# The last projections of 512 tokens: three kept weight tiles in two halves, or two passes over all eight tiles

## The chip, the cores and the metric

The kernel runs on one core of a Trainium2 chip. The metric is the device time of one execution in microseconds (us). A core has five engines, each of which works through its own instructions in order: TensorE (PE) for matmuls, VectorE (DVE), ScalarE (ACT), GpSimd (POOL) and SyncE (SP), which here issues nearly all DMAs. Engines wait for each other by semaphores.

## The reference

Two models of two layers each follow each other on 256 context and 256 latent tokens of width 1024, in float32. Cut to what the change touches, a layer is

```python
h = modulate(rms(x), shift, scale)            # context and latents have their own shift, scale, gate
x = x + gate * rms(mixer(h) @ w_out)          # second model: x + gate * (mixer(h) @ w_out)
h = modulate(rms(x), shift2, scale2)
x = x + gate2 * rms(ffn(h) @ w_down)          # second model: x + gate2 * (relu(h @ w1)**2 @ w2)
```

The mixers are gated linear attention with grouped attention, HGRN, latent attention with retention, and S5 (a state-space scan). The layers that still need the context compute w_out and w_down for all 512 tokens; the others for the 256 latents alone.

## The kernel before

Activations lie with the 1024 features on 8 x 128 partitions and the tokens in the free dimension, context in columns 0 to 255 and latents in 256 to 511. A float32 product is made of three matmuls of parts: `mm3` (L207) multiplies, for each block k of 128 input features, hi x xh, hi x xl and lo x xh, where hi is the rounded weight and lo its rest. `load` (L263) brings one weight tile, 128 output features by all of k, 512 KB (448 KB with seven blocks), by a DMA on SP into one of 4 `raw` buffers; `split` (L199) casts it to `hi` on ACT (L203) and subtracts to `lo` on DVE (L204), each with 3 buffers. The result of a tile goes to a bank of PSUM with the tag `pl`, of which there are 3, and `consume` evicts it from there.

`linear_steps` (L221) loops over the weight tiles. With `ends` set and N = 512 it does tiles 0 to 2 in two halves of 256 columns, tiles 3 and 4 at 512 columns, and then takes the last three together: it loads and splits them, does the context half of all three, calls `half()`, and does the latent half of all three. `half()` is where the context goes on while the latents are still being multiplied. Four places set `ends`:

- S1, about 344 to 400 us: `ew_out`, the output of the even mixer. `consume` copies to y (L1789) and adds the squares (`add_squares`: square L77 on ACT, sum by a matmul L85). `half()` is the first step of `halves` (L519): the rstd of the context's rows (cp L102, sums L105, eleven small DVE steps L420 to L428, spread over partitions by L119 on PE), then x += y * vecP * rstd tile by tile (L515 on DVE, L516 on GpSimd or DVE) with the squares of the new x. After the projection the same is done for the latents, and then the normalized X of both (L494 to L500), from which the ffn's matmuls read.
- S2, 790 to 836 us: `f0_d2`, the last of three down blocks of the first ffn, with seven blocks of k. `consume` adds to y (L1735). `half()` and what follows are as in S1.
- S3, 1711 to 1770 us: `bw_out`, the output of the second model's first mixer. `consume` (L1878) is x += gate * psum; x is loaded just before, from `ctx2` (L1872) and from the stored latents (L1873), into the place of tiles that the mixer used. M (L1046 on ACT, L1047 on DVE) is the mixer's output and the projection's input. `half()` is the context's rstd.
- S4, 2100 to 2149.6 us: `p0_d3`, the last of four down blocks of the third ffn. `consume` adds to y (L1735) and to x (L1909); `s5_collect` scales x to u (L1544), writes u of the tile to memory once its latent columns are there (L1547), and after tiles 3 and 7 gathers it back as U in eight DMAs (L1551). `s5_u` scales U (L1560, L1561), and the S5 scan (st, L1637 to L1641) works on what is computed from U.

The order of the instructions on each engine is not that of the code: a list scheduler sets it from priorities and dependences, and each engine then works in that order. Background streams that the loops advance with `tick` (here "w" and "m") have ended before these places' tiles are done.

## Time and profile before

| | us |
|---|---|
| median of three runs (2506.3 to 2512.42) | 2507.03 |
| the profiled execution's own time | 2504.24 |
| its span, first to last instruction | 2502.5 |
| PE busy in it | 2370.1 |
| DVE busy | 1499.1 |
| ACT busy | 967.3 |
| GpSimd busy | 453.7 |

The mean granted clock of TensorE is 0.971 of full speed. Busy times of engines overlap each other. A row of a timeline gives the start, the time, engine, line, operation, what is written and read, and, in brackets, how long the engine was idle before and what ended that; matmuls are pipelined, so their pace is the distance of their starts.

### The profile page before, as it was taken

Reading aid. Unit: us, or ns where it says so; the run is one execution under the profiler, and the core shown is the slowest. Engines: PE = TensorE matmul, PEld = TensorE weight load, DVE = VectorE, ACT = ScalarE, POOL = GpSimd, SP = SyncE. Lnnn points to the kernel's source line nnn. Section 1 sums busy time; section 2 is a strip of 40 time slices with the busy share of each in tenths; the row PEclk is TensorE's granted clock in tenths of the full one; section 3 lists DMA queues with packets and bytes.
Section 4 is the critical chain, followed back from the end, with each engine's and each line's share of the span. In section 5 each row is a group of like instructions: output and inputs, shape, how many; then the busy total and the mean of one; then the engine's idle time right before and its main releaser. Section 6 shows DMA issues by size and latency. Waiting matters only on the chain.

```text
span 2502.5 us, 40056 instructions
## 1 busy us (share of the span) xinstructions
PE 2370.1 (95%) x15813; PEld 1951.2 (78%) x15813; DVE 1499.1 (60%) x2913; ACT 967.3 (39%) x1591; POOL 453.7 (18%) x596
## 2 busy tenths in 40 slices
PE   7999988999999899999999999999999999958999
PEld 5875566888888669987899796557888888628999
DVE  5555446778853646674555633665688734586666
ACT  5523323322223434434444534443423224535543
POOL 3920012556630201101000100110000000360000
PEclk9999998999999899999999999999999999979999
DMA  8336671555552262225755431003365533966554
GB/s 301 114 101 227 228 278 59 162 165 168 158 154 93 80 210 76 72 81 182 264 177 181 160 108 59 9 18 119 118 188 179 165 97 109 221 253 210 168 180 150
DMA packets 162925, 378.05 MB, mean 151 GB/s; under 512 B 24144, under 2 KB 70096, under 8 KB 162608
## 3 DMA queue, kind: packets, MB, share of 16 engines
q1 hardware_dynamic: 159728, 368.27, 46.4%
q0 software_dynamic: 3008, 7.21, 1.0%
q8 instruction: 125, 2.05, 0.3%
q14 instruction: 64, 0.52, 0.1%
HBM read 344.75 MB, written 30.67 MB: 150 GB/s over the span
## 4 chain that ended last, share of the span: by engine, by line
PE 80%; DVE 10%; DMA 4%; ACT 3%; issue 2%; POOL 1%; SPq 0%; DVEq 0%; ACTq 0%; POOLq 0%
PE pl L213 19%; PE pl L214 18%; PE pl L215 18%; PE pm L337 3%; PE pl L993 2%; DVE lo L204 2%; DMA mcol<-ada_t 2%; PE pl L287 1%; PE pl L288 1%; PE pl L285 1%; DVE pm L403 1%; PE pa L669 1%; PE pb L1024 1%; PE pl L1015 1%; PE pa L85 1%
## 5 line engine op out<-in xcount | busy, mean ns | idle before, releaser
L203 ACT CAST hi<-raw 128x1024 fp32r<-128x1024 f32 (+4 forms) x393 | 400.6, 1020 | 841.5 <-PE pl L214 496.7
L204 DVE TENSOR_TENSOR lo<-raw,hi 128x1024 fp32r<-128x1024 f32 (+4 forms) x393 | 489.0, 1246 | 343.8 <-ACT hi L203 341.8
L214 PE MATMUL pl<-X,hi 128*128 128x256 f32 (+1 forms) x2032 | 646.4, 319 | 6.3 <-POOL X L498 5.8
L213 PE MATMUL pl<-X,hi 128*128 128x256 f32 (+1 forms) x2032 | 649.3, 322 | 2.0 <-ACT X L495 1.6
L215 PE MATMUL pl<-X,lo 128*128 128x256 f32 (+1 forms) x2032 | 644.5, 318 | 0.0
L214 PEld LDWEIGHTS pl<-X,hi 128*128 128x128 f32 x2032 | 390.1, 192 | 40.1 <-POOL X L498 8.3
L213 PEld LDWEIGHTS pl<-X,hi 128*128 128x128 f32 x2032 | 389.6, 193 | 40.3 <-issue 9.0
L215 PEld LDWEIGHTS pl<-X,lo 128*128 128x128 f32 x2032 | 389.8, 192 | 31.1 <-issue 4.9
L214 PE MATMUL pl<-hl,hi 128*128 128x256 f32 (+1 forms) x1071 | 327.2, 306 | 6.9 <-DVE hl L1722 6.8
L213 PE MATMUL pl<-hh,hi 128*128 128x256 f32 (+1 forms) x1071 | 327.7, 307 | 3.8 <-ACT hh L1721 3.7
L215 PE MATMUL pl<-hh,lo 128*128 128x256 f32 (+1 forms) x1071 | 325.8, 305 | 0.0
L213 PEld LDWEIGHTS pl<-hh,hi 128*128 128x128 f32 x1071 | 202.4, 189 | 19.8 <-ACT hh L1721 4.8
L214 PEld LDWEIGHTS pl<-hl,hi 128*128 128x128 f32 x1071 | 202.7, 189 | 18.5 <-DVE hl L1722 8.9
L215 PEld LDWEIGHTS pl<-hh,lo 128*128 128x128 f32 x1071 | 203.0, 190 | 10.3 <-issue 0.8
L337 PE MATMUL pm<-mraw,s_cc 128*32 128x512 f32 x576 | 119.2, 622 | 13.4 <-DMA mraw<-ada_w 13.1
L213 PE MATMUL pl<-M,hi 128*128 128x256 f32 (+1 forms) x416 | 122.9, 297 | 6.3 <-ACT hi L203 5.3
L1514 POOL TENSOR_TENSOR Ec<-PGr,bc 128x576 f32<-128x576 f32 x64 | 95.6, 1504 | 169.5 <-DMA bc<-s_w 87.5
L215 PE MATMUL pl<-M,lo 128*128 128x256 f32 (+1 forms) x416 | 122.2, 295 | 1.5 <-DVE lo L204 1.5
L214 PE MATMUL pl<-M,hi 128*128 128x256 f32 (+1 forms) x416 | 122.4, 296 | 0.2 <-DVE M L864 0.2
L498 POOL TENSOR_TENSOR X<-nt,X 128x256 fp32r<-128x256 f32 x48 | 37.9, 789 | 418.4 <-ACT nt L497 418.4
L403 DVE SCALAR_TENSOR_TENSOR pm<-mcol,mrow 128x512 f32<-128x512 f32 x128 | 89.3, 698 | 33.1 <-DMA mcol<-ada_t 22.8
L1735 DVE TENSOR_TENSOR y<-y,pl 128x256 f32<-128x256 f32 (+1 forms) x86 | 45.2, 526 | 102.5 <-PE pl L215 102.1
(513 smaller groups left out, 3629.6 us busy)
## 6 DMA issues: line engine op xcount, KB each, us to landing
mraw<-mod_w SPq DMA_DIRECT2D x96, 512.0 KB, 5.6
raw<-f_u SPq DMA_DIRECT2D x88, 512.0 KB, 4.3
mraw<-ada_w SPq DMA_DIRECT2D x64, 512.0 KB, 6.2
raw<-p_u SPq DMA_DIRECT2D x64, 512.0 KB, 3.7
raw<-p_d SPq DMA_DIRECT2D x64, 512.0 KB, 3.7
raw<-ow_fm SPq DMA_DIRECT2D x32, 512.0 KB, 3.3
mcol<-ada_t SPq DMA_DIRECT2D x64, 256.0 KB, 3.1
raw<-f_d SPq DMA_DIRECT2D x32, 448.0 KB, 3.3
```

The costliest lines, as they stand in the source:

```text
L85: K.nc.tensor.matmul(self.ps[32 * j:32 * j + 32, :N], K.ones[:rows, :32], sq[:rows, :N], start=k < 4, stop=k + 4 >= self.kt, skip_group_ch ...
L203: nc.scalar.copy(hi, raw)
L204: nc.vector.tensor_tensor(lo, raw, f32(hi), ALU.subtract)
L213: mm(out, w[0][:, kw, wsl], xh, start=first and a == 0, stop=False, skip_group_check=True)
L214: mm(out, w[0][:, kw, wsl], xl, start=False, stop=False, skip_group_check=True)
L215: mm(out, w[1][:, kw, wsl], xh, start=False, stop=last and a == nk - 1, skip_group_check=True)
L337: nc.tensor.matmul(ps[32 * j:32 * j + 32, :], s[:, k, :], raw[:, jj * 512:(jj + 1) * 512], start=k == 0, stop=k == KT - 1, skip_group_chec ...
L403: nc.vector.scalar_tensor_tensor(self.psum("pm"), buf[:, n % 2], 1.0, s[:, v], ALU.mult, ALU.mult, accum_out=(dst if h else part)[:, v, j: ...
L498: nc.gpsimd.tensor_tensor(lo[:, k, a:b], t, f32(hi[:, k, a:b]), ALU.subtract)
L993: nc.tensor.matmul(ps[:, :nk], q[:, tt * P:(tt + 1) * P], k[:, :nk], start=True, stop=True)
L1514: nc.gpsimd.tensor_tensor(Ec[i], ff[i], cs[i], ALU.mult)
L1735: nc.vector.tensor_tensor(y[:, c, a0:b0], y[:, c, a0:b0], ps, ALU.add)
```

## The change

With `ends`, the loop now makes two passes over all eight tiles: first the context half of each tile, then `half()`, then the latent half of each. Each pass loads and splits each tile itself and takes a bank for each half. The special case of the last three tiles goes. In `ffn` the flag is set where N is 512 alone, so that the ffns of 256 latents stay as they were.

```diff
--- before.py
+++ after.py
@@ -238,8 +238,18 @@
             self.mm3(ps[:M, :N], w, X, ks[early:], False, True, slice(0, M), slice(xoff, xoff + N))
             consume(first, ps[:M, :N], 0, N)
             yield
-        tail = nt - 3 if N == T and ends else nt
-        for c in range(1 if early else 0, tail):
+        if ends:
+            for a, b in ((0, CTX), (CTX, T)):
+                for c in range(nt):
+                    w, ps = weights(c), self.psum("pl")
+                    self.mm3(ps[:M, a:b], w, X, ks, True, True, slice(0, M), slice(xoff + a, xoff + b))
+                    consume(first + c, ps[:M, a:b], a, b)
+                    self.tick(tick)
+                    yield
+                if a == 0 and half is not None:
+                    half()
+            return
+        for c in range(1 if early else 0, nt):
             w = weights(c)
             ps = self.psum("pl")
             if N == T and c < 3:
@@ -250,15 +260,6 @@
             consume(first + c, ps[:M, :N], 0, N)
             self.tick(tick)
             yield
-        if tail < nt:
-            ws = [weights(c) for c in range(tail, nt)]
-            pss = [self.psum("pl") for _ in ws]
-            for a, b in ((0, CTX), (CTX, T)):
-                for i, (w, ps) in enumerate(zip(ws, pss)):
-                    part(ps, w, a, b)
-                    consume(first + tail + i, ps[:M, a:b], a, b)
-                if a == 0 and half is not None:
-                    half()
 
     def load(self, Wd):
         raw = self.wp.tile(list(Wd.shape), F32, tag="raw", name=self.n("raw"), bufs=4)
@@ -1737,7 +1738,7 @@
                     after(c, a0, b0)
 
             last = b == len(Wd) - 1
-            self.linear_fm(wd, (hi, lo), N, add, tick=ticks[1], ends=last, half=half if last else None)
+            self.linear_fm(wd, (hi, lo), N, add, tick=ticks[1], ends=last and N == T, half=half if last else None)
 
 
 def body(tc, A, out, dbg=None):
```

Instructions as the two kernels issue them: 13814 matmuls become 14000, DVE goes from 2787 to 2834, ACT from 1529 to 1561, SP from 833 to 865, GpSimd stays at 601. The orders of all engines differ inside S1 to S4 alone. Line numbers of the kernel after are one higher from L264 on.

S1 on DVE, from the subtraction of the sixth tile before, and of a tile of the second pass after (`Wt` is a product for the S5 weights, `cp` the start of the context's rstd, `y<-pl` an eviction). Before:

```order
L204 TENSOR_TENSOR lo_3149<-raw_3146,hi_3148 128x1024
L1506 TENSOR_TENSOR Wt_3736<-PGr,bc_3647 128x512
L1789 COPY y_2889<-pl_3074 128x512
L204 TENSOR_TENSOR lo_3155<-raw_3152,hi_3154 128x1024
L1789 COPY y_2889<-pl_3108 128x512
L204 TENSOR_TENSOR lo_3161<-raw_3158,hi_3160 128x1024
L1789 COPY y_2889<-pl_3164 128x256
L1789 COPY y_2889<-pl_3165 128x256
L1789 COPY y_2889<-pl_3166 128x256
L102 COPY cp_3253<-pa_2946 128x256
```

After:

```order
L204 TENSOR_TENSOR lo_3234<-raw_3231,hi_3233 128x1024
L1790 COPY y_2889<-pl_3101 128x256
L204 TENSOR_TENSOR lo_3269<-raw_3266,hi_3268 128x1024
L1507 TENSOR_TENSOR Wt_3758<-PGr,bc_3756 128x512
L1507 TENSOR_TENSOR Wt_3759<-PGr,bc_3756 128x512
L1790 COPY y_2889<-pl_3134 128x256
L1508 TENSOR_TENSOR Wt_3758<-Wt_3758,Wt_3759 128x512
L204 TENSOR_TENSOR lo_3302<-raw_3299,hi_3301 128x1024
L102 COPY cp_3169<-pa_2922 128x256
```

The two products `Wt` and their sum stand between evictions of the context's last tiles, and two subtractions and a sum ahead of `cp`.

S3 on DVE, from the last part of M (`M`) on; `x<-pl` is an eviction that needs x. Before:

```order
L1264 TENSOR_TENSOR rq_13319<-rq_13319,pb_15714 128x512
L1047 TENSOR_TENSOR M_14308<-rq_13319,M_14307 128x512
L204 TENSOR_TENSOR lo_15921<-raw_15918,hi_15920 128x1024
L1878 SCALAR_TENSOR_TENSOR x<-pl_15743,n_7567,x 128x256
L1878 SCALAR_TENSOR_TENSOR x<-pl_15806,n_7567,x 128x256
L204 TENSOR_TENSOR lo_15956<-raw_15953,hi_15955 128x1024
L1878 SCALAR_TENSOR_TENSOR x<-pl_15743,n_7567,x 128x256
L1878 SCALAR_TENSOR_TENSOR x<-pl_15806,n_7567,x 128x256
L1878 SCALAR_TENSOR_TENSOR x<-pl_15865,n_7567,x 128x256 x2
```

After:

```order
L1265 TENSOR_TENSOR rq_13531<-rq_13531,pb_15926 128x512
L1048 TENSOR_TENSOR M_14520<-rq_13531,M_14519 128x512
L204 TENSOR_TENSOR lo_16053<-raw_16050,hi_16052 128x1024
L204 TENSOR_TENSOR lo_16086<-raw_16083,hi_16085 128x1024
L204 TENSOR_TENSOR lo_16124<-raw_16121,hi_16123 128x1024
L1879 SCALAR_TENSOR_TENSOR x<-pl_15955,n_7779,x 128x256
L1879 SCALAR_TENSOR_TENSOR x<-pl_15990,n_7779,x 128x256
L1879 SCALAR_TENSOR_TENSOR x<-pl_16023,n_7779,x 128x256
L1879 SCALAR_TENSOR_TENSOR x<-pl_16056,n_7779,x 128x256
```

Three subtractions stand ahead of the first eviction, and the fourth tile's context half (`pl_16056`) is evicted right behind the first three.

S3 on PE, where the third tile ends and the fourth begins (the first three tiles are `pl_15743`, `pl_15806`, `pl_15865` before and `pl_15955`, `pl_15990`, `pl_16023` after). Before:

```order
L215 MATMUL pl_15865<-M_14307,lo_15862 128x256
L213 MATMUL pl_15865<-M_14307,hi_15861 128x256
L214 MATMUL pl_15865<-M_14308,hi_15861 128x256
L215 MATMUL pl_15865<-M_14307,lo_15862 128x256
L213 MATMUL pl_15924<-M_14307,hi_15920 128x512
L214 MATMUL pl_15924<-M_14308,hi_15920 128x512
```

After:

```order
L215 MATMUL pl_16023<-M_14519,lo_16020 128x256
L213 MATMUL pl_16023<-M_14519,hi_16019 128x256
L214 MATMUL pl_16023<-M_14520,hi_16019 128x256
L215 MATMUL pl_16023<-M_14519,lo_16020 128x256
L213 MATMUL pl_16056<-M_14519,hi_16052 128x256
L214 MATMUL pl_16056<-M_14520,hi_16052 128x256
```

Before, 92 matmuls, both halves of three tiles, stand between the first that needs the last part of M and the fourth tile; after, 20 do. Seven weight loads of this projection stand ahead of the loads of x on SP in both orders.

S4 on SP (`raw<-p_d` is a weight load, `u<-u` a written u, `U<-u` the gather, `wT` weights of S5). Before:

```order
L1547 DMA u<-u_19131 128x512
L265 DMA raw_19454<-p_d 128x1024
L1547 DMA u<-u_19131 128x512
L1619 DMA wT_20005<-tt 128x1024
L1547 DMA u<-u_19131 128x512
L1619 DMA wT_20015<-tt 128x1024
L1915 DMA xd<-x 128x4x256
L1547 DMA u<-u_19131 128x512
L1619 DMA wT_20025<-tt 128x1024
L1551 DMA U<-u 16x32x64 x8
L1547 DMA u<-u_19131 128x512 x4
```

After:

```order
L1548 DMA u<-u_19447 128x512
L266 DMA raw_20052<-p_d 128x1024
L1548 DMA u<-u_19447 128x512
L1620 DMA wT_20430<-tt 128x1024
L1548 DMA u<-u_19447 128x512
L1620 DMA wT_20440<-tt 128x1024
L1916 DMA xd<-x 128x4x256
L1548 DMA u<-u_19447 128x512
L1620 DMA wT_20450<-tt 128x1024
L1548 DMA u<-u_19447 128x512
L1552 DMA U<-u 16x32x64 x8
L1548 DMA u<-u_19447 128x512 x3
```

The fifth tile's u is now written ahead of the gather, and three are left behind it where four were; all weight loads of the second pass but the last stand ahead of the first u.

## Rows read from the trace of the kernel before

**Rows 1.** The page: busy time by engine; the chain's shares by engine.

```profile
PE 2370.1 (95%) x15813; PEld 1951.2 (78%) x15813; DVE 1499.1 (60%) x2913; ACT 967.3 (39%) x1591; POOL 453.7 (18%) x596
...
PE 80%; DVE 10%; DMA 4%; ACT 3%; issue 2%; POOL 1%; SPq 0%; DVEq 0%; ACTq 0%; POOLq 0%
```

**Rows 2.** Timeline of PE at S3: start, us, engine, line, tiles, [idle before].

```profile
1726.93 0.50 PE L213 MATMUL pl<-M,hi 128*128 128x256 f32 x2 [0.65 <-ACT M L1046]
...
1733.04 0.28 PE L214 MATMUL pl<-M,hi 128*128 128x256 f32 x1
...
1733.76 0.28 PE L214 MATMUL pl<-M,hi 128*128 128x256 f32 x1
...
1738.08 0.40 PE L213 MATMUL pl<-M,hi 128*128 128x512 f32 x1
...
1740.14 0.39 PE L213 MATMUL pl<-M,hi 128*128 128x512 f32 x1
```

**Rows 3.** Groups of ACT and DVE instructions by line: busy us, mean ns.

```profile
L203 ACT CAST hi<-raw 128x1024 fp32r<-128x1024 f32 x340 | 356.3, 1049 | 720.7 <-PE pl L214 450.1 <-issue 214.8 <-PE pl L288 25.8
...
L204 DVE TENSOR_TENSOR lo<-raw,hi 128x1024 fp32r<-128x1024 f32 x340 | 433.8, 1277 | 297.4 <-ACT hi L203 295.9
...
L1735 DVE TENSOR_TENSOR y<-y,pl 128x256 f32<-128x256 f32 x52 | 21.9, 421 | 36.7 <-PE pl L215 36.4
```

**Rows 4.** Timelines of DVE and, last, of PE at S1.

```profile
361.21 2.33 DVE L1506 TENSOR_TENSOR Wt<-PGr,bc 128x512 f32<-128x512 f32 x2 [0.18 <-DMA bc<-s_w]
...
365.17 1.20 DVE L1507 TENSOR_TENSOR Wt<-Wt,Wt 128x512 f32<-128x512 f32 x1
...
366.29 2.45 DVE L204 TENSOR_TENSOR lo<-raw,hi 128x1024 fp32r<-128x1024 f32 x1
...
418.34 0.62 PE L213 MATMUL pl<-X,hi 128*128 128x256 f32 x3 [0.51 <-ACT X L495]
```

**Rows 5.** Timelines of DVE, then of PE, behind S2's latent half.

```profile
840.04 0.16 DVE L420 TENSOR_SCALAR ms<-pb 128x2 f32<-128x2 f32 x1 [0.37 <-PE pb L105]
...
841.26 0.16 DVE L423 TENSOR_SCALAR ms<-ms 128x2 int32<-128x2 int32 x1
...
846.35 1.74 PE L85 MATMUL pb<-sq,ones 128*32 128x256 f32 x4 [1.82 <-ACT sq L77]
...
856.01 1.01 PE L213 MATMUL pl<-X,hi 128*128 128x256 f32 x3
```

**Rows 6.** Timelines of DVE and SP (DMA issues, SPq) at S3.

```profile
1726.91 0.69 DVE L1047 TENSOR_TENSOR M<-rq,M 128x512 fp32r<-128x512 f32 x1 [2.06 <-ACT M L1046]
...
1727.99 0.57 SPq L1872 DMA_DIRECT2D x<-ctx  x1
...
1733.75 0.93 DVE L1878 SCALAR_TENSOR_TENSOR x<-pl,n,x 128x256 f32<-128x256 f32 x2 [0.49 <-DMA x<-ctx]
```

**Rows 7.** PE's timeline; then the window: busy by engine, PEclk, DMA share, GB/s.

```profile
344.05 0.58 PE L213 MATMUL pl<-M,hi 128*128 128x256 f32 x1 [5.14 <-ACT hi L203]
...
344.00:350.00 6.00, 5.48 (x25) 5.19 (x26) 3.68 (x3) 2.10 (x2) 0.00 (x0) 0.53 0.79 259
```

**Rows 8.** SP and DVE timelines and one window behind S4's gathers.

```profile
2130.04 5.57 SPq L1551 DMA_DIRECT2D U<-u  x8
...
2140.00:2144.00 4.00, 4.00 (x32) 3.55 (x32) 2.40 (x12) 0.39 (x1) 0.00 (x0) 1.00 1.00 104
...
2149.56 0.42 DVE L1735 TENSOR_TENSOR y<-y,pl 128x256 f32<-128x256 f32 x1 [1.88 <-PE pl L215]
...
2153.78 8.50 SPq L1551 DMA_DIRECT2D U<-u  x8
...
2155.32 0.42 DVE L1560 TENSOR_TENSOR U<-U,pa 128x256 f32<-128x256 f32 x1 [0.18 <-DMA xd<-x]
...
2171.12 0.41 DVE L1560 TENSOR_TENSOR U<-U,pb 128x256 f32<-128x256 f32 x1
...
2173.14 0.50 DVE L1637 TENSOR_TENSOR st<-s5V,s5aa 128x256 f32<-128x256 f32 x1 [1.60 <-ACT s5V L1598]
```

## The prediction

> **What bounds the kernel now.** I read the page first: TensorE (PE) is busy 95% of a 2502.5 us span and 80% of the chain that ended last is PE [rows 1]. So what counts is PE's own instructions and the places where PE waits. The change touches four places, each one projection onto 512 tokens: S1, the output of the even mixer (about 344 to 400 us); S2, the last down block of the first ffn (790 to 836); S3, the output of the second mixer (1711 to 1770); S4, the last down block of the third ffn (2100 to 2149.6). At each I read the PE timeline for waits, then the timelines of the engine that PE waits for, then the order of the instructions before and after. The orders differ inside the four places alone, so I price these four and nothing else.
>
> **Matmuls.** In each place two tiles were done at 512 columns, 24 matmuls for a tile (21 at S2), and are now done in two halves of 256. In [rows 2] the 256-wide ones start 0.12 us apart (1733.04 to 1733.76, six steps) and the 512-wide ones 0.229 (1738.08 to 1740.14, nine steps), so a split costs 2 x 0.12 - 0.229 = 0.011 us. There are 24 x 2 x 3 + 21 x 2 = 186 such splits: 2.1 us, 0.5 in each place, all of it on PE. The Trainium skill (TensorE: Matmul & The Clock Gate, section "Wait — 56ns, not 53.3ns?") puts the spacing at columns over the clock and about 2.5 ns for each matmul; by that the 186 would cost 0.5 us and the sum below would be 1.6 us lower. The rows are of this kernel's own matmuls, and I keep theirs.
>
> **Second loads, casts and subtractions.** Each of the four places loads its eight tiles twice: 32 more loads, 32 casts on ScalarE (ACT, 1.05 us) and 32 subtractions on VectorE (DVE, 1.28 us) [rows 3]. A pass now takes PE 24 x 0.12 = 2.88 us for each tile; DVE needs 1.28 + 0.42 for a subtraction and half an eviction and ACT 1.05 and about as much as that eviction for a square [rows 3]. Both fit, so I price them at nothing by themselves; if the cover goes (a subtraction has taken 2.45 us beside GpSimd work at S1 [rows 4]), DVE's 2.45 + 0.42 just reaches 2.88. What costs is where such an instruction now stands ahead of one that PE waits for.
>
> **S1.** In the new order the weights' product for a later stage (two Wt instructions, 2.33 us; their sum 1.20) stands on DVE ahead of the eviction of the last context tile, and a subtraction ahead of the copy cp that starts the context's rstd chain. Counted from the end of the tile before, DVE has 0.42 + 1.28 + 2.33 = 4.0 us [rows 3, 4] of work against PE's 2.88; PE comes to the sum of squares 8 matmuls (0.96 us) into the latents, and needs an eviction and a square (0.42 each) more: about 1.0 us of waiting. The cp then stands behind 1.20 + 1.28 us while PE has 14 matmuls (1.7 us): 0.9. The rstd steps have another product, an eviction and a subtraction between them, which the 35 matmuls behind them (4.2 us) nearly cover: 0.3. S1: 0.5 + 1.0 + 0.9 + 0.3 = **+2.7** (bounds: 0 if nothing waits and the context's squares, done earlier, give back what the splits cost; +5 if two subtractions take 2.45).
>
> **S2.** One subtraction stood inside the latents' rstd chain: two steps that take 0.16 us start 1.22 us apart, at 840.04 and 841.26 [rows 5]; in the new order the subtraction is done by then, -1.0. On the other hand the sums of squares of the context's x now stand 12 matmuls behind the broadcast of rstd (L119) where they stood 24 behind. The way from L119 over DVE, GpSimd and ACT back to such a sum shows as 1.82 us of idle PE after the pass [rows 5]; twelve matmuls hide 1.4 of it, but DVE has a subtraction in between, so I take it whole, +1.8. S2: 0.5 + 1.8 - 1.0 = **+1.3** (bounds -0.5 and +3).
>
> **S3** is the largest term. The eviction here is x += gate x psum, and x is only loaded here: SP issues the load at 1727.99, behind DVE's M at 1726.91, and DVE has it at 1733.75 [rows 6]. PE gets the last part of M at 1726.93. Before, it then still has both halves of the first three tiles to do, 92 matmuls, and comes to the fourth tile at 1738.08 [rows 2]: the load is hidden. Now only the context half of three tiles stands there; 20 matmuls are left, done by 1726.93 + 20 x 0.12 = 1729.3. The fourth tile needs a bank, the projection has three, and the first comes free when x has landed and 0.48 us later: 1734.3. PE idles 5.0 us. S1 shows what such a hole does next: after 5.14 us of idle PE the granted clock of the next 6 us is 0.53, about the lower of its two levels (1.2 of 2.4 GHz), and 25 matmuls take 5.48 us in place of 3.0 [rows 7]: 2.5 us more. Seven loads of weights stand ahead of x on SP in both orders, so x itself comes no later. S3: 0.5 + 5.0 + 2.5 = **+8.0** (bounds +4.5 without the clock, +9.5).
>
> **S4.** After each latent tile u goes to memory, and after the fourth and the eighth tile a gather of eight DMAs brings U back. Before, all latent halves of the first five tiles come early: the first gather is issued from 2130.04 on, the DMA engines are still full at 2140 to 2144, so it takes some 13.5 us, and it is over when the last tile is evicted at 2149.56 [rows 8]. Now the fourth tile's latent half ends only four tiles (12 us) before the end, its gather is issued some 6.5 us before the end and, at 13.5 us is over about 7 us after it. The first use of U stood 5.8 us after the end (2155.32): +1.5. The last u is written behind that gather in SP's queue and lands about 8 us after the end; the second gather waits for it, was issued at 2153.78 before (4.2 after the end), and is 3.9 us later. Its user ends at 2171.5 and stands on DVE ahead of the scan's first step at 2173.14, which follows it: 1.6 us of slack, so +2.3. I take 2.5 for both together, since they overlap. S4: 0.5 + 0.3 (two more waits at the start) + 2.5 = **+3.3** (bounds +0.8, if the gather is quicker beside fewer loads, and +6, if the loads queued behind it come late for the chain too).
>
> **Sum.** 2.7 + 1.3 + 8.0 + 3.3 = 15.3 us. The profiled execution took 2504.24 us and would take 2519.5; the median of the three runs is 2.8 us above it, so on the median 2507.03 + 15.3 = **2522.3 us**, 0.6% slower.
>
> **Rivals.**
> (a) The two long terms are hidden: x lands before PE runs dry, or the fourth tile's matmuls find a bank, and the gather has slack in the scan. Then S3 is 0.5 and S4 0.8: 2.7 + 1.3 + 0.5 + 0.8 = 5.3, 2512.3 us, no change that can be told (0.3%, 7.5 us, is about what a measurement of this kernel can tell). For it speaks that PE had 11 us of cover before; against, that the order leaves 20 matmuls of it.
> (b) Faster: the latent pass of 23 us, where it was 8.6, hides the context's whole norm chain, so that PE does the context half of the next ffn's first three tiles (72 x 0.12 = 8.6 us) while it now idles after the pass until 418.34 [rows 4] and 856.01 [rows 5], and 3.5 us at S3's end. That is -20.8, with 2.1 + 7.5 + 2.8 still to pay: -8.4, 2498.6 us. It decides if the context's normalized tiles are written before the latents' rstd is asked for. Against it: in the new order these instructions stand on DVE and PE exactly where they stood, behind the latents' own.
> (c) Slower yet: the doubled subtractions meet the residual work on DVE and GpSimd in the latent passes of S1 and S2. If half of the 16 tiles see the 2.45 us, that is 8 x 1.2 = 10 us more: 2532 us. For it speaks [rows 4]; against, that GpSimd works in a few of these tiles only.
>
> **Chances.** Forecast 0.73, (a) 0.14, (b) 0.05, (c) 0.08. Faster by over 0.3%: (b), 0.05. Within 0.3%: (a) and the lowest corner of the forecast, 0.17. Slower: 0.78. The lower bounds of the four places add up to 0 - 0.5 + 4.5 + 0.8 = +4.8, the upper ones to 5 + 3 + 9.5 + 6 = +23.5, 2511.8 to 2530.5; with (a) and half of (c) inside the range is 2511 to 2532, which leaves out (b), the rest of (c) and a little more.
>
> **What would show it.** PE at S3: one idle stretch of about 5 us before the fourth tile, ended by DVE's eviction, and that by the DMA of x, with the clock at half speed behind it; if PE goes on there, S3 falls, and with it the forecast. At S4 the second use of U some 4 us later against the end of the projection, and the scan's first step 2 to 3 us later. At S1 and S2 waits of a microsecond or less at the sums of squares; waits for the subtraction itself tile after tile would be (c). A first ffn matmul that comes 8 us sooner after the pass would be (b).

## The result and the profile after

The changed kernel takes 2526.16 us (median of five runs, 2523.1 to 2531.12) against 2507.6 (2506.3 to 2516.51): a ratio of 1.0075 with a 95% interval of 1.0058 to 1.0093. It is 0.75% slower, 18.8 us (14.5 to 23.3); the forecast was 15.3 us and 2522.3. The same kernel, timed again later, gave 1.0063 [1.0041, 1.0086], 15.8 us.

The page of the changed kernel (its profiled execution took 2531.12 us, span 2529.3), busy time by engine, as the first row of [rows 1]:

```profile
PE 2382.2 (94%) x15999; PEld 1970.2 (78%) x15999; DVE 1542.6 (61%) x2960; ACT 999.3 (40%) x1623; POOL 450.8 (18%) x596
```

PE's busy time grew by 12.1 us and the span by 26.8, so more than half of the loss is PE waiting. DVE has 43.5 us more of work (47 instructions, most of them the second subtractions) and ACT 32.0.

**Where it went.** Two executions of the same code drift against each other, so spans don't tell what a place costs. I took the DVE and ACT instructions that both traces have in the same order, and the median difference of their start times in a stretch just ahead of each place and in one just behind it. What this difference grows by is the cost of the place:

| us | S1 | S2 | S3 | S4 |
|---|---|---|---|---|
| forecast | +2.7 | +1.3 | +8.0 | +3.3 |
| changed kernel | 5.4 | -0.5 | 6.9 | 0.6 |
| changed kernel, second time | 6.8 | -1.1 | 6.5 | 0.6 |

Places that an experiment (below) left as before came out between -1.2 and about +1, so about a microsecond of each number is noise. In stretches where nothing was changed the same difference wandered by several microseconds either way: ahead of S1 it lay between -2.3 and +5.9 in the traces of this study, and +5.5 of the 26.8 us by which this span is longer were there before S1 began.

One stretch of unchanged order does more than wander. Some 60 us behind S2's pass the difference grows by 3.0 us in the first trace of the changed kernel and by 1.9 in the second. PE's rows there, before and in the changed kernel, show a wait for a load of `ada_w`, the weights of the modulation:

```profile
899.64 1.92 PE L337 MATMUL pm<-mraw,s_cc 128*32 128x512 f32 x4 [2.32 <-DMA mraw<-ada_w]
```

```profile
913.97 1.92 PE L338 MATMUL pm<-mraw,s_cc 128*32 128x512 f32 x4 [4.29 <-DMA mraw<-ada_w]
```

The table counts none of this; the experiments show in which kernels it comes.

**S3** is as forecast. PE's timeline, as [rows 2]: start, us, engine, line, tiles, and in brackets the idle time before and what ended it:

```profile
1743.06 0.28 PE L215 MATMUL pl<-M,lo 128*128 128x256 f32 x1
1747.97 0.55 PE L213 MATMUL pl<-M,hi 128*128 128x256 f32 x1 [4.63 <-DVE x L1879]
1748.32 0.41 PE L214 MATMUL pl<-M,hi 128*128 128x256 f32 x1
1748.53 0.41 PE L215 MATMUL pl<-M,lo 128*128 128x256 f32 x1
```

The third tile's context half ends, PE finds no bank, and DVE's eviction frees one 4.63 us later. The eviction itself waits for the load of x, in the timelines of SP and DVE, as [rows 6]:

```profile
1741.43 0.57 SPq L1873 DMA_DIRECT2D x<-ctx  x1
...
1742.91 3.50 DVE L204 TENSOR_TENSOR lo<-raw,hi 128x1024 fp32r<-128x1024 f32 x3 [1.56 <-ACT hi L203]
...
1747.34 1.27 DVE L1879 SCALAR_TENSOR_TENSOR x<-pl,n,x 128x256 f32<-128x256 f32 x3 [0.93 <-DMA x<-ctx]
```

From issue to use it takes 5.91 us, where it was 5.76 [rows 6]: x comes no later, but PE comes earlier. DVE itself stands idle for x in the last 0.93 us only: until 1746.41 it does the three subtractions that the new order puts ahead of the first eviction. In this order an earlier x would have freed the bank at most 0.93 us sooner. And the clock falls behind the hole: the windows give busy us of PE, PEld, DVE, ACT and POOL, the granted clock, the DMA share and GB/s.

```profile
1743.00:1748.00 5.00, 0.37 (x4) 0.20 (x3) 4.07 (x5) 1.86 (x3) 0.00 (x0) 0.74 0.97 319
1748.00:1753.00 5.00, 5.00 (x26) 5.00 (x27) 0.63 (x3) 1.15 (x4) 0.00 (x0) 0.58 1.06 388
1753.00:1758.00 5.00, 5.00 (x46) 4.46 (x45) 3.31 (x4) 2.63 (x4) 0.00 (x0) 1.00 0.71 238
```

After 4.63 us of idle PE the clock of the second window is 0.58, near the lower of the two levels, and 26 matmuls are recorded in five microseconds where 46 follow in the next five.

**S1** cost twice the forecast. PE's waits in its two passes:

```profile
380.52 0.62 PE L85 MATMUL pa<-sq,ones 128*32 128x256 f32 x2 [1.79 <-ACT sq L77]
...
384.07 0.61 PE L105 MATMUL pa<-pack_sb,cp 128*128 128x1 f32 x4 [1.06 <-DVE cp L102]
...
390.79 0.68 PE L119 MATMUL pa<-pack_sb,rs 128*128 128x128 f32 x4 [1.82 <-DVE rs L429]
```

They are the three waits of the forecast, 4.67 us together where 2.2 were expected. The timelines of DVE and GpSimd beside them, as [rows 4], show why:

```profile
376.34 3.35 DVE L1507 TENSOR_TENSOR Wt<-PGr,bc 128x512 f32<-128x512 f32 x2
379.61 0.41 DVE L1790 COPY y<-pl 128x256 f32<-128x256 f32 x1
379.95 1.37 DVE L1508 TENSOR_TENSOR Wt<-Wt,Wt 128x512 f32<-128x512 f32 x1
381.24 2.45 DVE L204 TENSOR_TENSOR lo<-raw,hi 128x1024 fp32r<-128x1024 f32 x1
383.61 0.41 DVE L102 COPY cp<-pa 128x256 f32<-128x256 f32 x1
383.94 1.37 DVE L1507 TENSOR_TENSOR Wt<-PGr,bc 128x512 f32<-128x512 f32 x1
...
385.63 1.00 DVE L424 TENSOR_SCALAR ms<-ms 128x2 int32<-128x2 int32 x1
...
386.74 2.25 DVE L204 TENSOR_TENSOR lo<-raw,hi 128x1024 fp32r<-128x1024 f32 x1
```

```profile
375.23 5.54 POOL L1515 TENSOR_TENSOR Ec<-PGr,bc 128x576 f32<-128x576 f32 x3 [92.57 <-ACT hi L203]
380.73 1.87 POOL L1516 TENSOR_TENSOR Ec<-Ec,Ec 128x576 f32<-128x576 f32 x1
382.68 2.08 POOL L1515 TENSOR_TENSOR Ec<-PGr,bc 128x576 f32<-128x576 f32 x1
384.84 1.76 POOL L1516 TENSOR_TENSOR Ec<-Ec,Ec 128x576 f32<-128x576 f32 x1
386.68 1.24 POOL L1515 TENSOR_TENSOR Ec<-PGr,bc 128x576 f32<-128x576 f32 x1
```

GpSimd's products Ec, for the same S5 weights as Wt, stand in GpSimd's order where they stood. Before, they ran from 361.45 on, in the tiles of 512 columns, where PE waited for nothing; now they run from 375.23 to 387.92, over the last context tiles and most of the rstd chain. A DVE instruction that meets one ends a fixed time after it: the subtraction that starts at 381.24 ends at 383.69, 1.09 us after Ec's end at 382.60; the one of 386.74 ends at 388.99, 1.07 after 387.92; the product of 383.94 ends at 385.31, 0.55 after 384.76. So DVE waited until GpSimd was done, and then took nearly what it takes alone (the subtraction of 372.32, with no product beside it, took 1.23). In the kernel before, DVE met Ec too, and the distances are the same (1.08 for the subtraction of 366.29 [rows 4]); what is new is that PE waits for what stands behind. The Trainium skill (SBUF — State Buffer, section "Who interferes with whom") has a rule for it: a DVE instruction with two inputs in SBUF contends with a GpSimd instruction that reads SBUF, by a shared port pair that is locked exclusively, and one with at most one such input, outside the modes that use both port pairs, does not. The trace agrees for the instructions with two inputs and for the copies from PSUM between them, which keep their 0.41 us. But one step of the rstd chain with a single input in SBUF, L424, took 1.00 us in place of 0.17 (the median of its 34 in this trace) and ended 0.03 us behind the Ec of 384.84; whether it ran in such a mode the trace does not tell.

**S2.** The subtraction has left the latents' rstd chain, as forecast: the two steps that stood 1.22 us apart [rows 5] are 0.19 apart. PE waits in the passes 0.32 and 0.42 us, not the 1.8 that I took. DVE's timeline, and the longer of the two waits in PE's:

```profile
853.85 0.16 DVE L421 TENSOR_SCALAR ms<-pb 128x2 f32<-128x2 f32 x1 [0.37 <-PE pb L105]
854.04 0.17 DVE L424 TENSOR_SCALAR ms<-ms 128x2 int32<-128x2 int32 x1
```

```profile
832.91 1.30 PE L85 MATMUL pa<-sq,ones 128*32 128x256 f32 x4 [0.42 <-ACT sq L77]
```

**S4.** SP's issues of the two gathers, then DVE: the last eviction, the first use of each gather, and the first step of the scan, as [rows 8]:

```profile
2168.17 5.34 SPq L1552 DMA_DIRECT2D U<-u  x8
...
2181.63 6.10 SPq L1552 DMA_DIRECT2D U<-u  x8
```

```profile
2173.65 0.42 DVE L1736 TENSOR_TENSOR y<-y,pl 128x256 f32<-128x256 f32 x1 [1.89 <-PE pl L215]
...
2180.51 0.42 DVE L1561 TENSOR_TENSOR U<-U,pa 128x256 f32<-128x256 f32 x1 [1.29 <-DMA u<-u]
...
2193.48 0.42 DVE L1561 TENSOR_TENSOR U<-U,pa 128x256 f32<-128x256 f32 x1 [9.56 <-DMA s5aa<-aa]
...
2197.20 0.54 DVE L1638 TENSOR_TENSOR st<-s5V,s5aa 128x256 f32<-128x256 f32 x1 [0.98 <-ACT s5V L1599]
```

The first gather is issued 5.5 us before the last eviction and is first used 6.86 us after it (5.76 before); the second is issued 8.0 us after it (4.2 before), all as forecast. But the second is in use 11.85 us after its issue, where the one before took 15.02 (2153.78 to 2168.80; the row of 2193.48 names another load, but the gather's last part lands at 2193.40). So the scan starts 23.55 us after the last eviction, where it started 23.58 us after [rows 8].

### The profile page after: what moved, and what is told of

It is laid out like the page before. It is cut to its first block, busy times and chain, and to the rows that moved or that the text cites. A ratio compares the mean times of both kernels' runs of the same rounds, so it can differ in the third digit from the quotient of the medians.

```text
span 2529.3 us, 40631 instructions
## 1 busy us (share of the span) xinstructions
PE 2382.2 (94%) x15999; PEld 1970.2 (78%) x15999; DVE 1542.6 (61%) x2960; ACT 999.3 (40%) x1623; POOL 450.8 (18%) x596
## 4 chain that ended last, share of the span: by engine, by line
PE 78%; DVE 11%; DMA 5%; ACT 3%; issue 3%; POOL 1%; SPq 0%; DVEq 0%; ACTq 0%; POOLq 0%
PE pl L213 18%; PE pl L214 18%; PE pl L215 18%; PE pm L338 3%; PE pl L994 2%; DMA mcol<-ada_t 2%; DVE lo L204 2%; PE pl L288 1%; PE pl L289 1%; PE pl L286 1%; DVE pm L404 1%; PE pa L670 1%; PE pb L1025 1%; DMA mraw<-ada_w 1%; PE pl L1016 1%
## 5 line engine op out<-in xcount | busy, mean ns | idle before, releaser
L203 ACT CAST hi<-raw 128x1024 fp32r<-128x1024 f32 (+3 forms) x425 | 432.9, 1020 | 859.1 <-PE pl L214 506.8
L204 DVE TENSOR_TENSOR lo<-raw,hi 128x1024 fp32r<-128x1024 f32 (+3 forms) x425 | 525.6, 1239 | 365.8 <-ACT hi L203 358.4
L213 PE MATMUL pl<-hh,hi 128*128 128x256 f32 (+1 forms) x1101 | 333.7, 304 | 4.9 <-ACT hh L1722 4.8
L215 PE MATMUL pl<-hh,lo 128*128 128x256 f32 (+1 forms) x1101 | 331.3, 301 | 0.0
L213 PEld LDWEIGHTS pl<-hh,hi 128*128 128x128 f32 x1101 | 208.8, 190 | 19.7 <-ACT hh L1722 6.0
L214 PEld LDWEIGHTS pl<-hl,hi 128*128 128x128 f32 x1101 | 209.0, 190 | 19.4 <-DVE hl L1723 10.4
L215 PEld LDWEIGHTS pl<-hh,lo 128*128 128x128 f32 x1101 | 209.2, 190 | 9.8 <-issue 0.8
L213 PE MATMUL pl<-M,hi 128*128 128x256 f32 x448 | 130.3, 293 | 10.9 <-ACT hi L203 5.2
L338 PE MATMUL pm<-mraw,s_cc 128*32 128x512 f32 x576 | 117.8, 620 | 15.4 <-DMA mraw<-ada_w 15.0
L214 PE MATMUL pl<-M,hi 128*128 128x256 f32 x448 | 129.2, 290 | 0.2 <-DVE M L865 0.2
L215 PE MATMUL pl<-M,lo 128*128 128x256 f32 x448 | 128.9, 289 | 0.5 <-DVE lo L204 0.5
L404 DVE SCALAR_TENSOR_TENSOR pm<-mcol,mrow 128x512 f32<-128x512 f32 x128 | 89.3, 697 | 34.7 <-DMA mcol<-ada_t 23.3
L213 PEld LDWEIGHTS pl<-M,hi 128*128 128x128 f32 x448 | 87.8, 197 | 15.7 <-issue 7.7
```

The lines of the kernel that those rows point to most:

```text
L203: nc.scalar.copy(hi, raw)
L204: nc.vector.tensor_tensor(lo, raw, f32(hi), ALU.subtract)
L213: mm(out, w[0][:, kw, wsl], xh, start=first and a == 0, stop=False, skip_group_check=True)
L214: mm(out, w[0][:, kw, wsl], xl, start=False, stop=False, skip_group_check=True)
L215: mm(out, w[1][:, kw, wsl], xh, start=False, stop=last and a == nk - 1, skip_group_check=True)
L338: nc.tensor.matmul(ps[32 * j:32 * j + 32, :], s[:, k, :], raw[:, jj * 512:(jj + 1) * 512], start=k == 0, stop=k == KT - 1, skip_group_chec ...
```

## The experiments

Where an edit says `"keep"`, that place runs the loop of the kernel before: five tiles, then three kept ones in two halves. Each run was compared with the kernel before on the same chip; ratios have 95% intervals, and costs by place are taken as above.

**One place at a time.** In each of four kernels one place makes the two passes and the other three keep their tiles; a fifth is the changed kernel again. For S1 alone:

```diff
-            self.linear_fm(wd, (hi, lo), N, add, tick=ticks[1], ends=last and N == T, half=half if last else None)
+            self.linear_fm(wd, (hi, lo), N, add, tick=ticks[1], ends="keep" if last and N == T else False, half=half if last else None)
...
-            K.linear_fm(A["bw_out"], M, T, add, ends=True, half=lambda: bc.append(acc[0].rstd()))
+            K.linear_fm(A["bw_out"], M, T, add, ends="keep", half=lambda: bc.append(acc[0].rstd()))
```

S1 alone:

> S1 alone in two passes, S2 to S4 with three kept tiles. Theory: S1's waits come from its own order, so they are there without the other places: 5.3 us in the profile, 4 to 7 above before in the time. Rival: part of S1's price shows only with the others; 2 us or less.

S2 alone:

> S1, S3 and S4 with three kept tiles, S2 alone in two passes. Theory: S2 gives 0.7 us (its first to its last matmul is longer by less than the latents' rstd chain behind it is shorter), so the time is that of the kernel before within 3 us, 2504 to 2510; and the wait for a load of ada_w some 55 us behind S2 (4.29 us in the changed kernel, 2.32 before) differs from execution to execution. Rival (S2's second loads push later loads back): that wait is 4 us again and the time is 2 to 4 us above before.

S3 alone:

> S3 alone in two passes, the others with three kept tiles. Theory: the hole of 4.6 us and the stretch at half speed behind it, 6.8 us in the profile, 5 to 9 above before in the time. Rival: the gap is made up for in what follows, under 3.

S4 alone:

> S4 alone in two passes, the others with three kept tiles. Theory: the projection itself is 0.65 us longer; the first use of U comes 0.4 to 3 us later against its end, as the gather takes from execution to execution, and the scan starts 0 to 2.5 us later: 0.5 to 3 us above before, no change that can be told. Rival (the prediction's 3.3 us): 3 us or more, every time.

All four:

> The changed kernel once more, beside the three that follow. Theory (the change costs what its four places show: S1 5.3, S2 -1.0, S3 6.8, S4 1.3 us in the profiles so far, 12.4 in all, and what a profile shows beyond is the difference of single executions): 10 to 16 us above the kernel before. Rival (the change costs more than its places show, as the first five runs have it): 18 us or more above before.

| two passes at | us | ratio | cost by place, us |
|---|---|---|---|
| S1 | 2512.01 | 1.0016 [1.0000, 1.0032] | 5.7 |
| S2 | 2507.62 | 0.9999 [0.9983, 1.0015] | -1.0 |
| S3 | 2514.86 | 1.0027 [1.0014, 1.0041] | 7.1 |
| S4 | 2508.54 | 1.0005 [0.9989, 1.0020] | 0.0 |
| all four | 2523.6 | 1.0063 [1.0041, 1.0086] | 12.8 |

The four alone add up to 4.7 parts in a thousand, 11.8 us; all four together took 15.8 (10 to 22). Within the intervals the places may simply add, and two of them carry most of what can be seen: S3, and S1, whose interval by the whole time just reaches no change, but whose cost by place is 5.4 to 6.8 us in the four traces with two passes and this order there. The traces show a part that no single place has. The wait for `ada_w` behind S2 is 3.75 to 4.29 us in the five traces in which S1 and S2 both make two passes in the changed order, and 2.32 to 2.50 us in the seven in which at most one of them does; the difference of start times grows there by 1.6 to 3.8 us in the former and by -0.6 to +0.7 in the latter. So the expectation for S2 alone held (2.35 us), but the wait does not seem to differ by chance from execution to execution. That the two places together make it is read from these twelve traces after the fact; how they do was not tested.

**S1 kept, the rest changed.**

```diff
-            K.linear_fm(A["ew_out"], M, 512, mixed, ends=True, half=lambda: next(step))
+            K.linear_fm(A["ew_out"], M, 512, mixed, ends="keep", half=lambda: next(step))
```

> The changed kernel with S1 alone put back to three kept tiles in two halves. Theory (S1's price is DVE's queue: in the changed kernel PE waits there 1.79, 1.06 and 1.82 us for a square, for cp and for rstd): these three waits go, the stretch from the first matmul of S1 to the first of the ffn falls by 5 us, S2, S3 and S4 stay as in the changed kernel, and the time falls by about 5 us, to 2521. Rival (the price is the second loads, or lies in stretches whose order is unchanged): the time stays at 2526 within 2 us and S1 is no shorter than by the 0.5 us of its matmuls.

2515.49 us, 1.0033 [1.0014, 1.0052]: against the changed kernel's 1.0075 that is 4.2 parts in a thousand or 10.5 us back, more than the 5.4 that S1 cost in the trace; the two intervals leave room for less (1.0058 and 1.0052 are 1.5 us apart). Some 2 us of what is more lie in the wait for `ada_w`, which is 2.50 us here. By place S1 costs 0.8. S3 is untouched (a hole of 4.70 us, 7.1 by place). S4 costs 3.2, and shows what the forecast had in mind there:

```profile
2154.92 9.33 SPq L1572 DMA_DIRECT2D U<-u  x8
...
2161.45 0.42 DVE L1756 TENSOR_TENSOR y<-y,pl 128x256 f32<-128x256 f32 x1 [1.89 <-PE pl L215]
...
2170.19 0.42 DVE L1581 TENSOR_TENSOR U<-U,pa 128x256 f32<-128x256 f32 x1 [3.17 <-DMA u<-u]
...
2188.00 0.45 DVE L1658 TENSOR_TENSOR st<-s5V,s5aa 128x256 f32<-128x256 f32 x1
```

In this execution the first gather's issue took 9.33 us, its first use came 8.74 us after the last eviction and the scan 26.55 us after it, 3.0 later than before. So the term of S4 exists, but not in every execution: the same order of instructions gave 23.55 us in both traces of the changed kernel, and 23.29 where S4 alone was changed. The second gather is quicker in every trace with the changed order at S4: in use 11.2 to 13.5 us after its first issue in these six, 14.6 to 17.2 in the eight with the order of before.

**S3 without x.** The context's evictions at S3 copy the product to x, and the context part of x isn't loaded; gate and old x are left out of it.

```diff
-            nc.sync.dma_start(x[:, :, :CTX], A["ctx2"])
...
-                        nc.vector.scalar_tensor_tensor(x[:, i, a:b], ps[:, a - t0:b - t0], m0[:, v, 2, i:i + 1],
-                                                       x[:, i, a:b], ALU.mult, ALU.add)
+                        p = ps[:, a - t0:b - t0]
+                        if a:
+                            nc.vector.scalar_tensor_tensor(x[:, i, a:b], p, m0[:, v, 2, i:i + 1], x[:, i, a:b],
+                                                           ALU.mult, ALU.add)
+                        else:
+                            nc.vector.tensor_copy(x[:, i, a:b], p)
```

> The changed kernel; at S3 the context's eviction copies psum to x and x of the context isn't loaded (the context part of that residual sum is left out). Theory (the hole of 4.63 us is the load of x): the hole before the fourth tile is under 0.7 us, the clock stays at full speed behind it, and S3 is 6 to 7 us shorter; the time falls to about 2520. Rival (PE would have stopped there anyway, for the fourth tile's split weights, whose buffers come free with the first tile, or for the three banks): the hole keeps 2 us or more and the clock falls all the same.

2517.77 us, 1.0039 [1.0023, 1.0054]. S3's cost falls from 6.9 to 0.9 us by place. PE's next wait at this place, DVE's first evictions and the window behind them:

```profile
1734.53 0.51 PE L213 MATMUL pl<-M,hi 128*128 128x256 f32 x2 [0.65 <-ACT M L1047]
...
1735.80 0.76 DVE L1883 COPY x<-pl 128x256 f32<-128x256 f32 x2 [0.60 <-PE pl L215]
...
1735.00:1740.00 5.00, 4.98 (x41) 4.36 (x40) 4.20 (x7) 3.88 (x6) 0.00 (x0) 1.00 0.65 216
```

The wait for M, which was there before [rows 2], is all that is left, and the clock stays at its upper level. So the evictions' need of x makes the hole, and the hole makes the slow clock; without them the place costs what its splits cost, 0.5, and a little. But the edit changed DVE's order as well: here two evictions run ahead of the first subtraction, where in the changed kernel three subtractions (3.50 us) stood ahead of the first eviction. So the experiment takes away x and that order together; an earlier load alone, in the changed kernel's order, would save 0.93 us of the hole at most.

**S1 with the S5 products late.** A copy of one column makes the load of the array PG (read as PGr), from which Wt and Ec are made, wait for the first normalized tile, which lies behind S1:

```diff
+        nc.gpsimd.tensor_copy(PG[:, 0, 0, 0:1], f32(X[0][:, 0, 0:1]))
         nc.sync.dma_start(PG, sc["pg"])
...
-            K.bg["w"] = K.s5_weights(fp, sc)
+            K.bg["w"] = K.s5_weights(fp, sc, X)
```

> The changed kernel; the load of the powers from which the S5 weights (Wt on DVE, Ec on GpSimd) are made waits for the first normalized tile behind S1, so that none of these products lies in S1. Theory (S1's waits are these products: they stand on DVE ahead of an eviction and of cp, and while GpSimd works DVE's instructions take up to twice their time): the three waits of 4.7 us fall under 1.5 us together and S1 is about 4 us shorter; what the products cost later is not known, up to 3 us, so 2522 to 2526. Rival (the additional subtractions alone make the waits): waits of 3 us or more stay.

2524.12 us, 1.0069 [1.0048, 1.0089]: no gain. Yet the waits are gone, as they should be if the products make them: of the three one is left, 0.55 us, in PE's timeline:

```profile
378.69 1.30 PE L85 MATMUL pa<-sq,ones 128*32 128x256 f32 x4 [0.55 <-ACT sq L77]
```

From S1's first matmul to the first matmul of the ffn behind it it is 72.52 us here (342.18 to 414.70), 80.06 in the changed kernel (349.69 to 429.75) and 74.29 before (344.05 to 418.34). But then the products lie in the first tiles of the ffn. GpSimd, PE and a window there:

```profile
427.24 4.67 POOL L1516 TENSOR_TENSOR Ec<-PGr,bc 128x576 f32<-128x576 f32 x3
...
432.83 0.58 PE L214 MATMUL pl<-X,hi 128*128 128x256 f32 x1 [2.60 <-POOL X L499]
...
414.00:439.00 25.00, 19.78 (x116) 17.74 (x117) 18.24 (x40) 11.28 (x24) 16.47 (x16) 0.70 0.30 106
```

PE waits for normalized tiles that GpSimd makes behind them, the clock falls to 0.70, and by 440 us the place has cost 4.9 us after all. The products cause S1's waits; moved, they cause as much where they go. The edit moves Wt, which DVE computes, and Ec, which GpSimd computes, together, so it does not tell how much Wt's place in DVE's queue costs and how much the meeting with Ec.

**The faster rival, built.** Rival (b) needed the context's normalized tiles ahead of the latents' rstd, which the new order does not have. Four kernels, with S3 and S4 kept, give it to S1 and S2 or take parts of it away. "Early" writes the normalized context tiles within the half step (at S1 into the place of M's context half):

```diff
         self.residual_scaled(x, y, Pv, c, [accs[0].rstd()], new)
+        if early:
+            X = self.norm_tiles(T) if X is None else X
+            self.norm_scaled(X, x, Av, shift, c, [new[0].rstd()])
+            yield
...
```

"Late" is the edit to PG above, with the last normalized tile in place of the first.

Early, two passes at S1 and S2:

> S1 and S2 in two passes, S3 and S4 with three kept tiles; the context's normalized tiles within the latent pass at S1 and S2; the products for the S5 weights where the changed kernel has them, beside S1. Theory: S1's waits of 4.7 us beside the products stay, and put off the context's chain; PE still fills most of the stretch behind the pass: S1 3 to 6 us and S2 9 us shorter than before, 2492 to 2498. Rival: as in the version without the products, within 0.3% of before.

Early and late, two passes at S1 and S2:

> S1 and S2 in two passes, S3 and S4 with three kept tiles; at S1 and S2 the context's normalized tiles are computed in the half step, within the latent pass, and not behind the latents' (at S1 into the context half of M, whose columns are no longer read; at S2 into the tiles that the ffn's input leaves free); the products for the S5 weights start behind the last normalized tile of S1. Theory (what two passes offer is room for the context's whole norm chain, which the order of the changed kernel doesn't use): PE does the context half of three ffn tiles, 72 matmuls or 8.6 us, in the stretch in which it idles behind each of the two passes; with the waits for normalized tiles (3.3 us at S1) partly gone S1 is about 10 us and S2 about 9 us shorter than in the kernel before: 2485 to 2495. Rival (DVE, ScalarE and GpSimd are shared by both chains, so the latents' chain is put off by as much as PE gains): within 0.3% of before, 2500 to 2512.

Late alone, two passes at S1 and S2:

> S1 and S2 in two passes, S3 and S4 with three kept tiles; the products for the S5 weights start behind the last normalized tile of S1; the order of the norms is that of the changed kernel. Theory (S1's price in the changed kernel was the products beside it): S1 is no longer than with three kept tiles, and the time is that of the control without the passes within 3 us, 2501 to 2507. Rival (second loads and subtractions cost by themselves): 5 us or more above the control.

Late alone, all four places kept:

> All four places with three kept tiles, as before; only the products for the S5 weights start behind the last normalized tile of S1. A control for the others. Theory: PE's waits for normalized tiles behind S1, 3.3 us before, fall to 1 us or so, the products have slack until S2: 2 to 3 us less than before, 2504 to 2506. Rival: the products come too late for S2's half step, and the time rises by what they lack.

| | us | ratio |
|---|---|---|
| early | 2518.64 | 1.0045 [1.0029, 1.0061] |
| early, late | 2512.51 | 1.0020 [1.0004, 1.0035] |
| late | 2514.33 | 1.0028 [1.0015, 1.0040] |
| late, all kept | 2512.16 | 1.0022 [1.0009, 1.0035] |

None is faster than the kernel before. Three windows over 70 us of it, from the kept tiles on to the ffn's first tiles, and the answering three of "early":

```profile
374.00:400.00 26.00, 25.84 (x197) 20.95 (x197) 11.94 (x32) 8.06 (x17) 3.85 (x5) 1.00 0.26 84
400.00:419.00 19.00, 12.76 (x61) 6.25 (x55) 14.99 (x49) 6.69 (x17) 3.89 (x5) 0.73 0.21 69
419.00:444.00 25.00, 21.25 (x154) 19.77 (x155) 17.00 (x37) 14.74 (x28) 10.07 (x11) 0.93 0.14 37
```

```profile
378.90:404.90 26.00, 22.57 (x145) 16.80 (x145) 19.93 (x38) 9.61 (x19) 11.24 (x10) 1.00 0.38 121
404.90:423.90 19.00, 18.78 (x147) 16.49 (x147) 14.87 (x42) 9.24 (x19) 4.67 (x4) 1.00 0.36 116
423.90:448.90 25.00, 17.34 (x107) 12.81 (x107) 19.11 (x47) 9.84 (x22) 12.79 (x13) 0.76 0.21 58
```

The rival's mechanism works: behind the pass PE is busy 18.78 of 19 us at full clock, where it was 12.76 at 0.73. It gains 6 us there, loses 3.3 ahead of it in S1's waits and 3.9 behind it: 58.7 busy microseconds of 70, where it was 59.9 (399 recorded matmuls, where there were 412). What PE waits for at the end is this:

```profile
445.69 0.58 PE L214 MATMUL pl<-M,hi 128*128 128x256 f32 x1 [3.51 <-POOL M L519]
```

It is the low part of a normalized latent tile. PE has used up the work that it could do meanwhile, and the latents' last tile comes no sooner. The two kernels with late products show it: counted from S1's first matmul, the latents' last eviction comes after 62.6 us in "early, late" and 57.1 in "late", and the way from there to the last normalized tile takes 25.3 and 30.5 us, so that this tile is done after 87.8 and 87.6 us. What the early chain saves behind the pass it adds within it, and the idle time has moved behind. By place, S1 costs 5.6 us in "early" and 5.7 where S1 alone is changed.

At S2, where no S5 products lie, "early" fills the gap as well. The windows behind S2's pass, before and in "early":

```profile
836.00:856.00 20.00, 13.12 (x52) 5.82 (x49) 14.06 (x48) 6.76 (x18) 3.89 (x6) 0.63 0.42 133
```

```profile
847.70:867.70 20.00, 18.96 (x137) 15.14 (x136) 16.52 (x40) 9.97 (x23) 7.19 (x9) 1.00 0.31 107
```

Again it is lost behind, and more than that: at 892 and 920 us PE waits 3.01 and 3.26 us for loads of `ada_w`, and by 960 us of the kernel before the place has cost 5.1 us in "early" and 5.8 in "early, late", where it is 0.7 in "late".

Putting the S5 products late costs in the same way: with all places kept ("late, all kept") PE waits 1.37, 2.22 and 1.63 us at 444 to 452 us for Wt and Ec themselves, and in the 30 us from 444.7 it is busy 26.07 at a clock of 0.83, where before, from 444, it was busy all 30 at 1.00. By place that is 3.9 us.

"Late" against "late, all kept" shows what two passes at S1 and S2 cost where the products are out of the way: 2.2 us by the medians, which the intervals cannot tell from nothing, and by place at S1 4.2 against 3.9 us. So the 5.7 us of S1 come with the products and not with the second loads and subtractions alone. "Early, late" against "late" shows what the early chain is worth once the products are out of its way: 1.8 us, less than the intervals can tell from nothing.

## Why the prediction was right, and where its terms were off

The forecast named the right sign and the loss at S3 with its cause, and the time lies 3.9 us above it, within the range. The terms:

- **Splits, second loads and casts.** PE's busy time grew by 12.1 us, part of it at the lower clock, so the 2.1 us of 186 splits can't be read alone. S2 alone, with 42 of them, costs nothing that shows. The spacing of the Trainium skill (TensorE: Matmul & The Clock Gate, section "Wait — 56ns, not 53.3ns?") would make them 0.5 us, an estimate, and no run here tells the two sums apart.
- **S1, +2.7: mis-sized, it is about 5.7.** The step that failed priced two Wt at 2.33 us, from where they ran before, and subtractions at their mean of 1.28. They took 3.35, 2.45 and 2.25, since GpSimd's Ec products, which ran beside the wide tiles before, now run beside these. The forecast left GpSimd, whose order is unchanged, out of the sum, but what matters is when the products run against the rstd chain. It had the row (a subtraction of 2.45 [rows 4]) and used it as a bound only; that bound, +5, is close to what came. The third wait is 1.82, not 0.3: a product and a slowed subtraction stand among its steps. (The second, by the prediction's own terms, would be 0.8 and not 0.9.) The experiments with the products late show that the products make the waits; that the slowing by Ec, and not Wt's own place, makes the excess over the forecast is read from the prices in the trace and was not tested apart.
- **S2, +1.3: about nothing.** The gain of 1.0 in the rstd chain came. The wait of 1.8 did not: I took the whole way back from L119 because DVE had a subtraction on it, though twelve matmuls hide 1.4; 0.32 and 0.42 us show. That is the lower of the two values between which the prediction chose. What comes with S2 when S1 is changed too, the longer wait for `ada_w` behind it, is in no term.
- **S3, +8.0: about 7.** The hole is 4.45 to 4.79 us in the five traces that have it, against 5.0, the clock behind it is at 0.58, and without x in the context's evictions the place costs 0.9. The wait, what ends it and its price through the clock are as forecast. What the forecast did not count are the three subtractions on DVE ahead of the eviction. It lost nothing by that, since x comes 0.93 us behind them, but without any wait for x this order would still leave 3.7 us of the hole (4.63 less 0.93).
- **S4, +3.3: about 1, from 0 to 3.2.** The gathers moved as forecast, to the microsecond. What failed is the last step, in which the second gather was to take as long as it had taken before. It took 11.85 us from issue to first use where that one took 15.02, which makes up for most of its being issued 3.8 us later, and it is quicker in all six traces with this order (11.2 to 13.5 us). The prediction had a quicker gather as the lower bound of this term, +0.8, and named fewer loads beside it as the reason; the reason was not tested. (The first use of U, by its own terms, would be 1.2 later and not 1.5.)
- **Rival (a)** does not hold: S3's load is not hidden. **Rival (b)** does not hold in the change, since the instructions stand where they stood, and, built, it does not give the 20.8 us: that sum counted the stretch that is filled and not that the latents' last normalized tile comes no sooner. **Rival (c)** named what came on top at S1, but in S1's context pass and its chain, not tile after tile in the latent passes: S2 is free of it.

The errors of S1 (3.0 too low), S2 (2.0 too high), S3 (1 too high) and S4 (2.3 too high) partly cancel: by places 12.4 and 12.8 us in the two traces of the changed kernel, where 15.3 were forecast. The whole times, 18.8 and 15.8 us with intervals of 14.5 to 23.3 and 10 to 22, are above both. The stretch with the wait for `ada_w` adds 3.0 and 1.9 us, 15.4 and 14.7 in all, which both intervals hold. So that the sum came out so close is luck in part: three terms too high, one too low, and one cost that the forecast did not have. For the rest, drift between executions of up to 5 us in stretches that the change leaves alone is enough, but that was not tested.

## What to carry to other kernels

When an order changes, ask first what each transfer had for cover: a load that was hidden by 92 matmuls is bare behind 20, and the hole of 4.63 us cost 1.8 us more through the clock (20 matmuls 0.21 us apart in place of 0.12). Price an instruction not by what it took before but by what will run beside it, on DVE above all by what GpSimd does then, even if GpSimd's order does not change. And a gap that is filled at one place will show at the next one, as long as the chain behind it ends no sooner: count PE's busy time over the whole stretch, not in the gap alone. And look behind the places that were changed: of the two passes' price 2 to 3 us came at a load some 60 us behind the second of them.

## What the runs showed of the hardware

- DVE and GpSimd take turns, exactly: three DVE instructions end 1.07 to 1.09 (subtraction) or 0.55 us (product) after the GpSimd instruction that they met, and the GpSimd product that follows one has 2.08 us where one that began first has 1.24. The three that met one in the kernel before ended 1.08, 0.54 and 1.08 us behind. A step with one input in SBUF and 2 elements a row was held too, 1.00 us in place of 0.17.
- Idle stretches of one length can cost clock or not. At S1 PE idled 2.73 us in the second trace of the changed kernel and 2.74 us where S1 alone was changed, both times before the same sum of squares. In the first the clock of the 8 us from 378.43 was 0.57, in the other that from 375.36 was 1.00. Their windows, in that order:

```profile
378.43:386.43 8.00, 7.68 (x39) 7.39 (x40) 7.22 (x14) 1.05 (x1) 5.23 (x3) 0.57 0.49 138
```

```profile
375.36:383.36 8.00, 6.95 (x55) 6.44 (x53) 7.83 (x15) 2.02 (x2) 5.51 (x4) 1.00 0.48 132
```

- In the first of these the waits at S1 add up to 3.26 us and in the changed kernel's first trace to 4.67, and yet S1 cost more in it (6.8 and 5.4): the clock took what the later waits gave back. What decides between the two is not told by these runs.
- The DMAs of the same gather, 128 KB each, had a median of 7.3 to 8.2 us from issue to landing in the eight traces with the order of before at S4, and in the six with the changed order of 5.6 to 6.4 in five and 7.8 in the sixth, the one in which S4 cost 3.2 us. It goes with the order, but what in it makes the difference was not found.
